# The last products of a stage in parts of the tokens, their norms and consumers part by part; the inverse's z times V with 128 columns

## The chip, the cores and the metric

The kernel runs on one core of one Trainium2 chip, as one program of some 56,700 instructions on the engines. The metric is the device time of one execution in microseconds (us): the median of the runs shown below. The engines are named as in the profile: PE is TensorE's matmuls and PEld its weight loads, DVE is VectorE, ACT ScalarE, POOL GpSimd, SP SyncE, which issues the DMAs.

## The reference, cut to what matters

Two residual blocks with adaptive norms work on 512 latent tokens and 256 context tokens of width 1024:

```python
def modulate(x, shift, scale):
    return rms_norm(x) * (1.0 + scale) + shift

def squared_relu_mlp(h, w1, w2):
    return jnp.square(jax.nn.relu(h @ w1)) @ w2
...
        h_l = modulate(x, sh_a, sc_a)
        h_c = modulate(ctx, csh_a, csc_a)
        if layer % 2 == 0:
            o_l, o_c = ab_mixer(h_l, h_c, ...)
        else:
            o_l, o_c = rwkv_mixer(h_l, h_c, ...)
        x = x + gt_a * o_l
        x = x + gt_m * squared_relu_mlp(modulate(x, sh_m, sc_m), mlp_w1[layer], mlp_w2[layer])
        if need_ctx:
            ctx = ctx + cgt_a * o_c
            ctx = ctx + cgt_m * squared_relu_mlp(modulate(ctx, csh_m, csc_m), mlp_w1[layer], mlp_w2[layer])
```

Layer 0 mixes with neighbourhood attention and an mLSTM (ab_mixer), layer 1 with an RWKV7 scan (rwkv_mixer), whose context output is not needed. A second block with another context follows (its mixer, and a mixture of experts), which the change touches at its first norm only. Every mixer ends in a product with a 1024x1024 matrix, every MLP in one with 4096x1024; its result is added to x, and the next stage begins with the norm of the new x.

## The kernel before, in words

All activations stand transposed: x is eight tiles (k = 0 to 7) of 128 features x 768 tokens, the latents in columns 0 to 511, the context in 512 to 767. `PARTS` is these two ranges, `LAT` the first alone. The stages follow each other: ab_mixer (its last products are called po), mlp(0) (products up and dn), rw_mixer (first products rp, the scan, last products ro), mlp(1) (latents only: up, dn), second_block (first products p).

A weight tile is 128 outputs x 1024 inputs in f32. `load_w` (L479) fetches it with a DMA into one of three buffers (wraw) and splits it into a rounded part wh on ACT (L476) and the rest wl on POOL (L477), each with two buffers. `dense` (L489) then runs, for each of the eight k, three products (wh with the activation's high part, wh with its low part, wl with the high part), each over every range of `parts`: 48 matmuls for `PARTS`, 24 for `LAT`. `dense_pair` does the first two weights of a stage at once, k by k, because its activations appear tile by tile.

The last products of a stage: for each output tile f, `dense`, then `residual` on DVE (L589, x += ps * gate) and `squares_add`: a square on ACT (L544) and the sum over f in acc (L546), on POOL for all f but the last. `rstd_tokens` sums acc over the partitions on PE (ssc, L554) and takes the reciprocal root (rsv, rst, rsy; L518 to L534); `rstd_banks` spreads it over the partitions by six products (rstd, L564). `modulate` then makes, k by k, modt on DVE (L579), ah on ACT (L581) and al on DVE (L582); these feed the pair of the next stage. In rw_mixer `shift` stands there: x scaled in place on DVE (L1138), shifted on ACT (L1140), and the sum of the two neighbouring tokens xx on POOL (L1141, with an edge copy on either side, L1142 and L1143); `tiles` makes the products' tiles from x and xx.

In rw_mixer the scan inverts 64x64 matrices block by block; the l-th step multiplies z with V (L1669): the weights are `U[:, c, :]`, 64 columns of f16, for each of 12 matrices c.

The order of instructions on each engine is set when the program is built: the code is written stage by stage, and a scheduler places the instructions of all engines by its own model of their times. Each engine then runs its list in order and waits at semaphores.

## Time and profile before

| | |
|---|---|
| median of 3 runs | 3540.41 us (3536.74 to 3541.11) |
| the profiled execution | 3541.96 us, its span 3540.1 us |
| PE busy | 3200.3 us (90%), 23582 matmuls |
| DVE, ACT, POOL busy | 1822.3 us (51%), 1321.4 us (37%), 910.1 us (26%) |
| wh on ACT, wl on POOL | 259 each, 1032 and 2410 ns |
| PE busy in 530 to 578 us (po) | 48.00 of 48 us, granted clock 1.00 |
| PE busy in 578 to 608 us (norm 1) | 23.16 of 30 us, clock 0.77 |
| PE busy in 1152 to 1194 us (norm 2) | 26.34 of 42 us, clock 0.72 |
| PE busy in 2233 to 2256 us (norm 3) | 16.34 of 23 us, clock 0.78 |
| PE busy in 2632 to 2664 us (norm 4) | 26.38 of 32 us, clock 0.79 |

PE is nearly always busy in the dense stretches, and pauses at the norms between two stages. The four norms that the change touches are numbered in order of time: 1 after po, 2 after dn of mlp(0), 3 after ro, 4 after dn of mlp(1). The granted clock is the share of TensorE's full speed that it ran at.

### The profile page before, as it was taken

What the parts mean: (1) busy time and instruction counts of PE and PEld (TensorE: products, weight loads), DVE (VectorE), ACT (ScalarE), POOL (GpSimd) and SP (SyncE); (2) the same over time, 40 slices, a digit from 0 to 9 for tenths busy, and PEclk for the clock granted to TensorE, in tenths of its full rate; (3) what the DMA queues carried; (4) which work ended last, traced back from release to release, by engine and by line L of the source; (5) the groups of instructions that cost most, each with busy time, mean ns of one, the idle gap of its engine ahead of it and who ended that gap; (6) DMA issues with size and microseconds to landing.
All of it is one profiled execution on the core that took longest, in us unless ns stands there. A gap on an engine that the chain in (4) does not pass through costs nothing. (4 is left out here: it accounts for less than half of the span.)

```text
span 3540.1 us, 56694 instructions
## 1 busy us (share of the span) xinstructions
PE 3200.3 (90%) x23582; PEld 2423.1 (68%) x23582; DVE 1822.3 (51%) x3073; ACT 1321.4 (37%) x2503; POOL 910.1 (26%) x467
## 2 busy tenths in 40 slices
PE   7989999999999789589999998899999989799887
PEld 4666887788888677377777786677878767433333
DVE  5476664852322975477777763774342564222213
ACT  3333453221222543377777775322233453100001
POOL 1111113222223423422222221444442324200000
PEclk9999999999999899699999998999999999899999
DMA  5222222551112223200000003474231227799997
GB/s 219 96 71 84 84 78 90 198 176 61 65 60 97 84 106 109 69 18 27 27 28 27 27 8 105 154 245 136 95 124 54 78 81 247 261 426 426 426 427 321
DMA packets 126321, 488.44 MB, mean 138 GB/s; under 512 B 13360, under 2 KB 23024, under 8 KB 101744
## 3 DMA queue, kind: packets, MB, share of 16 engines
q1 hardware_dynamic: 119936, 477.25, 36.6%
q8 instruction: 186, 3.05, 0.3%
q10 hardware_dynamic: 4944, 3.36, 0.3%
q0 software_dynamic: 1184, 4.20, 0.3%
q14 instruction: 71, 0.58, 0.0%
HBM read 455.92 MB, written 28.84 MB: 137 GB/s over the span
## 5 line engine op out<-in xcount | busy, mean ns | idle before, releaser
L477 POOL TENSOR_TENSOR wl<-w,wh 128x1024 fp32r<-128x1024 f32 (+1 forms) x259 | 623.5, 2410 | 1614.1 <-ACT wh L476 1461.6
L476 ACT ACTIVATE wh<-w 128x1024 fp32r<-128x1024 f32 (+1 forms) x259 | 266.9, 1032 | 920.3 <-PE dn L498 335.6
L498 PE MATMUL dn<-hh,wh 128*128 128x512 f32 (+1 forms) x768 | 236.4, 362 | 15.1 <-ACT hh L476 15.1
L498 PE MATMUL up<-ah,wh 128*128 128x512 f32 (+1 forms) x768 | 236.9, 364 | 6.5 <-ACT ah L581 2.8
L498 PE MATMUL up<-ah,wl 128*128 128x512 f32 (+1 forms) x768 | 236.6, 362 | 6.1 <-POOL wl L477 5.9
L498 PE MATMUL dn<-hl,wh 128*128 128x512 f32 (+1 forms) x768 | 236.7, 362 | 2.2 <-DVE hl L477 2.2
L498 PE MATMUL dn<-hh,wl 128*128 128x512 f32 (+1 forms) x768 | 235.8, 361 | 1.1 <-POOL wl L477 1.1
L498 PE MATMUL up<-al,wh 128*128 128x512 f32 (+1 forms) x768 | 236.6, 362 | 0.2 <-DVE al L582 0.2
L465 DVE SCALAR_TENSOR_TENSOR side<-wside,condb 128x1024 f32<-128x1024 f32 x128 | 193.2, 1509 | 66.7 <-DMA wside<-ada 65.4
L621 DVE TENSOR_TENSOR u<-u 128x768 f32<-128x768 f32 (+1 forms) x64 | 126.7, 1982 | 133.4 <-ACT u L620 133.4
L589 DVE SCALAR_TENSOR_TENSOR x<-dn,ada,x 128x512 f32<-128x512 f32 x96 | 60.5, 658 | 260.4 <-PE dn L498 260.4
L498 PEld LDWEIGHTS dn<-hh,wh 128*128 128x128 f32 x768 | 128.5, 190 | 40.4 <-ACT hh L476 16.6
L498 PEld LDWEIGHTS up<-ah,wh 128*128 128x128 f32 x768 | 128.9, 191 | 32.5 <-ACT ah L581 3.9
L498 PEld LDWEIGHTS up<-ah,wl 128*128 128x128 f32 x768 | 128.3, 190 | 33.3 <-POOL wl L477 9.9
L498 PEld LDWEIGHTS dn<-hl,wh 128*128 128x128 f32 x768 | 128.4, 190 | 28.0 <-DVE hl L477 4.3
L498 PEld LDWEIGHTS up<-al,wh 128*128 128x128 f32 x768 | 129.0, 191 | 25.2 <-DVE al L582 1.4
L498 PEld LDWEIGHTS dn<-hh,wl 128*128 128x128 f32 x768 | 128.3, 190 | 25.7 <-POOL wl L477 2.0
L476 ACT ACTIVATE hh<-u 128x768 fp32r<-128x768 f32 (+1 forms) x64 | 47.3, 740 | 220.1 <-DVE u L621 220.1
L498 PE MATMUL p<-ah,wh 128*128 128x512 f32 (+1 forms) x320 | 118.7, 400 | 2.2 <-ACT ah L581 1.2
L498 PE MATMUL rp<-xl,wh 128*128 128x512 f32 x368 | 110.2, 364 | 10.2 <-DVE xl L477 10.2
L498 PE MATMUL rp<-xh,wh 128*128 128x512 f32 x368 | 110.1, 366 | 9.1 <-ACT xh L476 7.8
L498 PE MATMUL p<-ah,wl 128*128 128x512 f32 x320 | 113.6, 384 | 2.1 <-POOL wl L477 2.1
(623 smaller groups left out, 7459.7 us busy)
## 6 DMA issues: line engine op xcount, KB each, us to landing
w<-mlp SPq DMA_DIRECT2D x128, 512.0 KB, 3.5
wside<-ada SPq DMA_DIRECT2D x96, 512.0 KB, 3.8
ew<-e_gate SPq DMA_DIRECT2D x45, 1024.0 KB, 19.5
ew<-e_up SPq DMA_DIRECT2D x41, 1024.0 KB, 20.7
ew<-e_down SPq DMA_DIRECT2D x39, 1024.0 KB, 19.5
wada<-ada SPq DMA_DIRECT2D x48, 512.0 KB, 3.8
ewm<-e_up SPq DMA_DIRECT2D x18, 1024.0 KB, 19.6
ewm<-e_down SPq DMA_DIRECT2D x18, 1024.0 KB, 19.6
```

The source lines that it names most:

```text
L465: nc.vector.scalar_tensor_tensor(o, w, 1.0, cb[:, q, :], op0=ALU.mult, op1=ALU.mult, accum_out=out[:, f, q:q + 1])
L476: nc.scalar.activation(hi, src, AF.Copy)
L477: (eng or nc.vector).tensor_tensor(lo, src, hi.bitcast(F32), op=ALU.subtract)
L498: nc.tensor.matmul(ps[:, a:b], ww[:, 128 * k:128 * k + 128], aa[:, a:b], start=(first and k == 0 and q == 0), stop=(last and k == nk - 1 a ...
L589: self.nc.vector.scalar_tensor_tensor(x[:, a:b], ps[:, a:b], gt[:, f, q:q + 1], x[:, a:b], op0=ALU.mult, op1=ALU.add)
L621: nc.vector.tensor_tensor(u[:, lo:hi], u[:, lo:hi], u[:, lo:hi], op=ALU.mult)
```

## The change

The last products of the four stages run part by part: all eight f for the first part, then all eight for the second. At po and dn of mlp(0) the parts are the latents and the context (`PARTS`), at ro and dn of mlp(1) the two halves of the latents (`HALVES`). So each of those weights is loaded and split twice. Each part has its own squares (the sums of 256 columns on DVE instead of POOL), ssc, rsqrt and rstd; those of the first part stand in the second part's products. `dense_pair`, `modulate`, and shift and tiles of rw_mixer (now `first_tiles`) go through a first part of all k, then the second. At norm 4 the context's norm is done ahead of the dn products. x is saved to DRAM for rw_mixer's end after the first part of mlp(0)'s last products, and its latents only. Two small constants move from a tile of the whole program to one of ab_mixer. In the scan, V has 13 matrices instead of 12, and z times V takes `U[:, c:c + 2]`, 128 columns, as weights; of the 128 partitions of its result 64 are read, as before.

```diff
+HALVES = ((0, T // 2), (T // 2, T))
...
+    def spill_x(self, part):
+
+        if part[0] < T:
+            for k in range(KD):
+                self.nc.sync.dma_start(self.dxs[k], self.x[k][:, :T])
...
         ps = [self.wide(name) for _ in srcs]
-        for k in range(n // 128):
-            for p, w in zip(ps, ws):
-                self.dense(p, [t[:, 128 * k:128 * k + 128] for t in w], act, parts, k0=k, first=(k == 0), last=(k == n // 128 - 1))
+        for part in parts:
+            for k in range(n // 128):
+                for p, w in zip(ps, ws):
+                    self.dense(p, [t[:, 128 * k:128 * k + 128] for t in w], act, [part], k0=k, first=(k == 0),
+                               last=(k == n // 128 - 1))
...
-    def modulate(self, tiles, sh, sc1, parts, pool):
+    def modulate(self, tiles, sh, sc1, pool):
...
+        for n, ((a, b), r) in enumerate(self.r.items()):
+            q = int(a >= T)
+            for k in range(KD):
+                t = pool.tile([128, TT], F32, tag="tmp", name=self.uid("modt"), bufs=self.tb)
+                if n == 0:
+                    out.append([pool.tile([128, TT], F32R, tag=tag, name=self.uid(tag), bufs=KD) for tag in ("ah", "al")])
+                h, l = out[k]
+                nc.vector.scalar_tensor_tensor(t[:, a:b], tiles[k][:, a:b], sc1[:, k, q:q + 1], r,
                                                op0=ALU.mult, op1=ALU.mult)
                 nc.scalar.activation(h[:, a:b], t[:, a:b], AF.Identity, bias=sh[:, k, q:q + 1])
                 nc.vector.scalar_tensor_tensor(l[:, a:b], t[:, a:b], sh[:, k, q:q + 1], h[:, a:b].bitcast(F32),
                                                op0=ALU.add, op1=ALU.subtract)
...
+    def residual_parts(self, name, product, gt, parts, acc, tmp, step=None, hook=None):
+
+        y = None
+        for n, part in enumerate(parts):
+            for f in range(KD):
+                ps = product(n, f, part)
+                self.residual(self.x[f], ps, gt, f, [part])
+                self.squares_add(acc, self.x[f], f, [part], tmp, self.nc.gpsimd if part[1] - part[0] > 256 else None)
+                if step:
+                    step()
+                if n and f == 1:
+                    self.r[parts[0]] = self.rstd_banks(y, parts[:1])[0]
+            y = self.rstd_tokens(acc, [part])
+            if hook:
+                hook(part)
+        self.r[parts[1]] = self.rstd_banks(y, parts[1:])[0]
...
+                    if layer == 1:
+
+                        for k in range(KD):
+                            self.squares_add(acc, self.x[k], k, PARTS[1:], tmp)
+                        self.r[PARTS[1]] = self.rstd_banks(self.rstd_tokens(acc, PARTS[1:]), PARTS[1:])[0]
+
+                    def product(n, f, part):
+                        ps = self.wide("dn")
+                        self.dense(ps, self.load_w(w2[g, f], 1024), hid, [part])
+                        return ps
+
+                    self.residual_parts("dn", product, gt, nparts, acc, tmp, next_side, hook)
+                    break
...
-            for f in range(KD):
+
+            def product(n, f, part):
                 ps = self.wide("po")
-                self.dense(ps, self.load_w(wo[f], 1024), act2, PARTS)
-                self.residual(self.x[f], ps, self.ada[0, 2], f, PARTS)
-                self.squares_add(acc, self.x[f], f, PARTS, tmp, nc.gpsimd)
-            self.y = self.rstd_tokens(acc, PARTS)
+                self.dense(ps, self.load_w(wo[f], 1024), act2, [part])
+                return ps
+
+            self.residual_parts("po", product, self.ada[0, 2], PARTS, acc, tmp)
...
-                for k in range(KD):
-                    nc.sync.dma_start(spill["x"][k], self.x[k])
...
+                def shift(k, q):
+                    h, s = hs[k], xx[k]
+                    for a, b in PARTS[q:q + 1]:
                         nc.vector.scalar_tensor_tensor(h[:, a:b], self.x[k][:, a:b], sc[:, k, q:q + 1], r[q],
                                                        op0=ALU.mult, op1=ALU.mult)
                         nc.scalar.activation(h[:, a:b], h[:, a:b], AF.Identity, bias=sh[:, k, q:q + 1])
                         (nc.gpsimd if k else nc.vector).tensor_tensor(s[:, a + 1:b - 1], h[:, a:b - 2], h[:, a + 2:b], op=ALU.add)
                         nc.gpsimd.tensor_copy(s[:, a:a + 1], h[:, a + 1:a + 2])
                         nc.gpsimd.tensor_copy(s[:, b - 1:b], h[:, b - 2:b - 1])
...
+                def first_tiles():
+
+                    out = []
+                    for q, (a, b) in enumerate(PARTS):
+                        n = 0
+                        for k in range(KD):
+                            while n < min(k + 3, KD):
+                                shift(n, q)
+                                n += 1
+                            t = pool.tile([128, TT], F32, tag="tmp", name=self.uid("xs"), bufs=self.tb)
+                            if q == 0:
+                                out.append(pair())
+                            h, l = out[k]
+                            nc.scalar.activation(t[:, a:b], hs[k][:, a:b], AF.Copy, scale=m2[:, 1, k:k + 1])
+                            nc.vector.scalar_tensor_tensor(t[:, a:b], xx[k][:, a:b], m2[:, 0, k:k + 1], t[:, a:b],
+                                                           op0=ALU.mult, op1=ALU.add)
+                            self.split(t[:, a:b], h[:, a:b], l[:, a:b])
+                    return out
...
-                first = self.dense_pair("ro", [wo[0], wo[1]], act, LAT, ws)
+                first = self.dense_pair("ro", [wo[0], wo[1]], act, HALVES[:1], ws)
...
+                self.residual_parts("ro", product, gt, HALVES, acc, tmp)
...
-                    nc.tensor.matmul(pz[:64, 64 * (c - a):64 * (c - a) + 64], U[:, c, :],
+                    nc.tensor.matmul(pz[:, 64 * (c - a):64 * (c - a) + 64], U[:, c:c + 2, :].rearrange("p c t -> p (c t)"),
                                      zb[:, c].rearrange("p h (b x w) -> p h b x w", x=2, w=w)[:, :, :, 1, :],
...
-        k.mlp(0, PARTS)
+        k.mlp(0, PARTS, PARTS, k.spill_x)
         k.rw_mixer()
-        k.mlp(1, PARTS[:1])
+        k.mlp(1, PARTS[:1], HALVES)
```

Line numbers of the changed kernel: L502 matmul of dense, L480 wh and other ACT splits, L481 wl, L546 and L550 squares on ACT, L552 acc, L524 to L540 rsqrt, L586 and L589 modulate, L596 residual, L1074 to L1149 the mLSTM head. Three places of the order follow. First PE, while the last mLSTM head finishes (ho are its last products, which need hsum from DVE; ch and cl are the activations of po, of which tile 7 needs ho). Before:

```order
L498 MATMUL po_4651<-ch_4555,wl_4655 128x512
L498 MATMUL po_4651<-ch_4555,wl_4655 128x256
L498 MATMUL po_4651<-ch_4559,wh_4654 128x512
L1103 MATMUL ho_4533<-consts,hsum_4489 128x128 x3
L498 MATMUL po_4651<-ch_4559,wh_4654 128x256
L1103 MATMUL ho_4533<-consts,hsum_4489 128x128
L1103 MATMUL ho_4539<-consts,hsum_4489 128x128
L498 MATMUL po_4651<-cl_4560,wh_4654 128x512
L1103 MATMUL ho_4539<-consts,hsum_4489 128x128
L498 MATMUL po_4651<-cl_4560,wh_4654 128x256
L498 MATMUL po_4651<-ch_4559,wl_4655 128x512
```

and the same place of the change:

```order
L502 MATMUL po_4644<-ch_4585,wh_4647 128x512
L502 MATMUL po_4644<-cl_4586,wh_4647 128x512
L502 MATMUL po_4644<-ch_4585,wl_4648 128x512
L1149 MATMUL ho_4551<-consts,hsum_4507 128x128 x4
L1149 MATMUL ho_4557<-consts,hsum_4507 128x128 x2
L502 MATMUL po_4610<-ch_4589,wh_4613 128x512
L502 MATMUL po_4644<-ch_4589,wh_4647 128x512
L502 MATMUL po_4610<-cl_4590,wh_4613 128x512
L502 MATMUL po_4610<-ch_4589,wl_4614 128x512
```

Before, 84 po matmuls of both widths (f0 and f1, k 0 to 6) stand ahead of or around ho; in the change it is 42 of 512 columns, all of them ahead, and behind ho come the products that need tile 7. Second DVE at norm 1, from the last residuals of po to the first modulated tiles. Before:

```order
L589 SCALAR_TENSOR_TENSOR x_4581<-po_4951,ada_2_356,x_4581 128x256
L589 SCALAR_TENSOR_TENSOR x_4582<-po_5011,ada_2_356,x_4582 128x512
L589 SCALAR_TENSOR_TENSOR x_4582<-po_5011,ada_2_356,x_4582 128x256
L546 TENSOR_TENSOR acc_4591<-acc_4591,sq_5068 128x768
L518 TENSOR_SCALAR rsv_5078<-ssc_5071 128x6
L527 RECIPROCAL rsy_5079<-rst_5081 128x6
L531 TENSOR_TENSOR rst_5081<-rsy_5079 128x6
L532 TENSOR_TENSOR rst_5081<-rst_5081,rsv_5078 128x6
L533 TENSOR_SCALAR rst_5081<-rst_5081 128x6
L534 TENSOR_TENSOR rsy_5079<-rsy_5079,rst_5081 128x6
L579 SCALAR_TENSOR_TENSOR modt_5104<-x_4575,ada_4_357,rstd_5096 128x512
L579 SCALAR_TENSOR_TENSOR modt_5104<-x_4575,ada_4_357,rstd_5101 128x256
```

and the change:

```order
L596 SCALAR_TENSOR_TENSOR x_4599<-po_5118,ada_2_374,x_4599 128x256
L552 TENSOR_TENSOR acc_4609<-acc_4609,sq_5150 128x256
L596 SCALAR_TENSOR_TENSOR x_4600<-po_5153,ada_2_374,x_4600 128x256
L552 TENSOR_TENSOR acc_4609<-acc_4609,sq_5185 128x256
L524 TENSOR_SCALAR rsv_5191<-ssc_5188 128x2
L586 SCALAR_TENSOR_TENSOR modt_5214<-x_4593,ada_4_375,rstd_4973 128x512
L533 RECIPROCAL rsy_5192<-rst_5194 128x2
L586 SCALAR_TENSOR_TENSOR modt_5220<-x_4594,ada_4_375,rstd_4973 128x512
L537 TENSOR_TENSOR rst_5194<-rsy_5192 128x2
L589 SCALAR_TENSOR_TENSOR al_5216<-modt_5214,ada_3_376,ah_5215 128x512
L538 TENSOR_TENSOR rst_5194<-rst_5194,rsv_5191 128x2
```

In the change the second part's residuals and sums follow one another, and the first modulation of 512 columns (modt_5214, which needs rstd of the first part only) stands behind the last sum and rsv of the second part. Third ACT at norm 4, where dn of mlp(1) begins. Before:

```order
L620 ACTIVATE u_25824<-up_25793 128x512
L476 ACTIVATE hh_25825<-u_25824 128x512
L476 ACTIVATE wh_25903<-w_25901 128x1024
L540 ACTIVATE acc_25831<-x_23186 128x768
L541 ACT_TABLE_LOAD
L541 ACTIVATE warm<-acc_25831 128x1
L476 ACTIVATE wh_25938<-w_25936 128x1024
L544 ACTIVATE sq_25898<-x_23187 128x768
```

and the change:

```order
L649 ACTIVATE u_26439<-up_26408 128x512
L546 ACTIVATE acc_26446<-x_23428 128x256
L550 ACTIVATE sq_26449<-x_23429 128x256
L547 ACT_TABLE_LOAD
L547 ACTIVATE warm<-acc_26446 128x1
L480 ACTIVATE hh_26440<-u_26439 128x512
L550 ACTIVATE sq_26452<-x_23430 128x256
L550 ACTIVATE sq_26455<-x_23431 128x256
L550 ACTIVATE sq_26458<-x_23432 128x256
L550 ACTIVATE sq_26461<-x_23433 128x256
L550 ACTIVATE sq_26464<-x_23434 128x256
L480 ACTIVATE wh_26558<-w_26556 128x1024
```

The squares of the context tiles (all of 256 columns, acc_26446 to sq_26464) now stand ahead of wh_26558, the third weight of dn.

## Rows read from the trace of the kernel before

**Rows 1.** Timeline of PE at the start of po (start, duration, work, [idle <-releaser]).

```profile
519.59 0.62 PE L1103 MATMUL ho<-consts,hsum 128*128 128x128 f32 x3
```

**Rows 2.** Timeline of DVE: residuals of po, then of dn of mlp(1).

```profile
569.83 1.14 DVE L589 SCALAR_TENSOR_TENSOR x<-po,ada,x 128x512 f32<-128x512 f32 x2 [7.34 <-PE po L498]
...
578.31 1.14 DVE L589 SCALAR_TENSOR_TENSOR x<-po,ada,x 128x512 f32<-128x512 f32 x2 [7.34 <-PE po L498]
...
2592.07 0.75 DVE L589 SCALAR_TENSOR_TENSOR x<-dn,ada,x 128x512 f32<-128x512 f32 x1 [0.82 <-PE dn L498]
...
2597.67 0.75 DVE L589 SCALAR_TENSOR_TENSOR x<-dn,ada,x 128x512 f32<-128x512 f32 x1 [4.85 <-PE dn L498]
```

**Rows 3.** Timeline of ACT and POOL: one weight's split during po.

```profile
569.52 1.06 ACT L476 ACTIVATE wh<-w 128x1024 fp32r<-128x1024 f32 x1 [6.15 <-PE po L498]
...
570.66 2.40 POOL L477 TENSOR_TENSOR wl<-w,wh 128x1024 fp32r<-128x1024 f32 x1 [4.29 <-ACT wh L476]
```

**Rows 4.** Timelines at norm 1.

```profile
579.14 2.35 POOL L477 TENSOR_TENSOR wl<-w,wh 128x1024 fp32r<-128x1024 f32 x1 [4.29 <-ACT wh L476]
...
580.43 1.87 DVE L546 TENSOR_TENSOR acc<-acc,sq 128x768 f32<-128x768 f32 x1 [0.98 <-ACT sq L544]
...
582.35 2.72 PE L554 MATMUL ssc<-ones,acc 128*128 128x2 f32 x12 [4.08 <-DVE acc L546]
...
587.75 1.80 DVE L579 SCALAR_TENSOR_TENSOR modt<-x,ada,rstd 128x512 f32<-128x512 f32 x3 [1.21 <-PE rstd L564]
...
607.75 1.06 ACT L476 ACTIVATE wh<-w 128x1024 fp32r<-128x1024 f32 x1 [2.79 <-PE up L498]
```

**Rows 5.** Groups by form, 588 to 606 us (count | busy us, mean ns | idle).

```profile
L582 DVE SCALAR_TENSOR_TENSOR al<-modt,ada,ah 128x512 fp32r<-128x512 f32 x8 | 6.0, 746 | 0.0
...
L582 DVE SCALAR_TENSOR_TENSOR al<-modt,ada,ah 128x256 fp32r<-128x256 f32 x8 | 3.8, 479 | 0.0
...
L581 ACT ACTIVATE ah<-modt,ada 128x256 fp32r<-128x256 f32 x8 | 4.0, 500 | 2.9 <-DVE modt L579 2.8
```

**Rows 6.** Timelines at norm 2.

```profile
1151.71 1.14 DVE L589 SCALAR_TENSOR_TENSOR x<-dn,ada,x 128x512 f32<-128x512 f32 x2 [7.33 <-PE dn L498]
...
1171.03 1.03 POOL L1141 TENSOR_TENSOR xx<-x 128x510 f32<-128x510 f32 x1
...
1173.81 0.61 POOL L1141 TENSOR_TENSOR xx<-x 128x254 f32<-128x254 f32 x1
...
1174.61 1.03 POOL L1141 TENSOR_TENSOR xx<-x 128x510 f32<-128x510 f32 x1
...
1193.80 1.06 ACT L476 ACTIVATE wh<-w 128x1024 fp32r<-128x1024 f32 x1 [3.12 <-PE rp L498]
```

**Rows 7.** Timelines at norm 3.

```profile
2232.46 0.75 DVE L589 SCALAR_TENSOR_TENSOR x<-ro,ada,x 128x512 f32<-128x512 f32 x1 [4.69 <-PE ro L498]
...
2255.60 1.06 ACT L476 ACTIVATE wh<-w 128x1024 fp32r<-128x1024 f32 x1 [6.04 <-issue]
```

**Rows 8.** Timelines at norm 4 and in its products.

```profile
2593.72 1.28 ACT L541 ACT_TABLE_LOAD   x1
...
2631.26 0.75 DVE L589 SCALAR_TENSOR_TENSOR x<-dn,ada,x 128x512 f32<-128x512 f32 x1 [4.85 <-PE dn L498]
...
2663.29 1.06 ACT L476 ACTIVATE wh<-w 128x1024 fp32r<-128x1024 f32 x1 [2.97 <-PE p L498]
```

**Rows 9.** Lines L1669 and L1635 (duration min/median/max), and their timeline.

```profile
L1669 PEld LDWEIGHTS <-V x960: 106/113/177, 1481.2 to 2128.9; 128*64 128x64 f16 x192
...
L1635 PEld LDWEIGHTS <-zb x384: 95/98/152, 1476.1 to 2131.0; 128*128 128x128 f16 x192
...
1515.22 0.44 PE L1669 MATMUL i<-zb,V 128*64 128x64 f16 x8
...
1503.33 0.52 PE L1635 MATMUL i<-crwh,zb 128*128 128x64 f16 x12
```

**Rows 10.** Timeline of POOL in mlp(0), two wl in a row.

```profile
608.94 5.96 POOL L477 TENSOR_TENSOR wl<-w,wh 128x1024 fp32r<-128x1024 f32 x2 [27.46 <-ACT wh L476]
```

More of the change, by code (lines that the diff above doesn't have):

```diff
@@ L334, in __init__ @@
         nc.vector.memset(self.eps, 1e-6)
+        dr = ctx.enter_context(tc.tile_pool(name="x_d", bufs=1, space=bass.MemoryType.DRAM))
+        self.dxs = [dr.tile([128, T], F32, name=f"d_x{k}") for k in range(KD)]
         self.warm = self.const.tile([128, 1], F32, name="warm")
@@ L597, in mlp @@
         with tc.tile_pool(name=f"mlp{layer}", bufs=2, reuse_waits="tile") as pool:
+            for tag, dt, bufs in (("hh", F32R, 10), ("hl", F32R, 10)):
+                pool.tile([128, TT], dt, tag=tag, name=self.uid(tag), bufs=bufs)
             side = self.ada_side(layer + 1, pool)
@@ L626, in up, with next_side @@
                 return hid
+            def next_side():
+                if side:
+                    side.pop(0)()
             if layer == 1:
@@ L1122, in rw_mixer @@
             H = {n: crh[:, a:b] for n, (a, b) in self.crwh.items()}
-            spill = {n: [dr.tile([128, TT], F32, name=f"d_{n}{f}") for f in range(8)] for n in ("x", "r", "k", "kk", "v", "g", "o")}
+            spill = {n: [dr.tile([128, TT], F32, name=f"d_{n}{f}") for f in range(8)] for n in ("r", "k", "kk", "v", "g", "o")}
             tw = [cp.tile([128, TT], F32R, name=f"tw{z}") for z in range(2)]
@@ L1341, in rw_scan @@
             hi=[diag(f"hi{i}", dt=F16) for i in range(2)], zb=[diag(f"zb{i}", dt=F16) for i in range(2)], lo=diag("lo", dt=F16),
-            V=[pool.tile([128, 12, 64], F16, name=f"V{l}", bufs=1) for l in range(1, 6)],
+            V=[pool.tile([128, 13, 64], F16, name=f"V{l}", bufs=1) for l in range(1, 6)],
             C=C, H=H, tw=tw, ta=ta, pool=pool, n=0)
```

109 lines of the change are left out of this document (45 added, 64 removed).

## The prediction

> **What bounds the kernel now.** The kernel is a chain of dense stages, so I first read the timeline of the engines around the four norms that the change touches. In a dense stretch TensorE never waits: one 128x1024 weight over 768 tokens takes 8.48 us (569.83 to 578.31, two results apart), one over 512 tokens 5.60 us (2592.07 to 2597.67) [rows 2]. So the 256 context tokens of a weight cost 2.88 us. The supply of weights has slack there: ScalarE makes the high half (wh) as soon as TensorE frees a buffer, at 569.52, GpSimd the low half (wl) from 570.66 to 573.06 [rows 3], 3.54 us after the release and well inside 8.48 or 5.60.
>
> At a norm the chain breaks. The last residual of the first one starts at 578.31 [rows 2]; the last addition of squares waits behind GpSimd, the statistics start on TensorE at 582.35, the first modulated tile at 587.75, and the pair of products after it gives its first buffer back at 607.75 [rows 4]: 29.4 us for 17.0 us of products. The other three, from the last residual to that release: 42.1 us [rows 6], 23.1 us [rows 7], 32.0 us [rows 8].
>
> **What the change costs: the products.** Every weight of the four stages comes twice, and the second pass runs over 256 tokens only. With two buffers a release starts wh and wl (3.54 us), and 22 of 24 matmuls still follow from the first that needs wl (2.88 x 22/24 = 2.64 us): 6.18 us for two weights, 3.09 for one, against 2.88 us of work. In order:
> - Norm 1 (po): 8 such weights x 0.21 = 1.7 us. The statistics of the first part stand 19 matmuls into the next weight, in front of the other 29, and need GpSimd's addition first; by their count they take two thirds of the 2.72 us of all twelve [rows 4], some of it under the running matmuls: I take 1.4 us. And the run-ahead shrinks: while the last mLSTM head finishes, until ho at 519.59 [rows 1] and somewhat beyond, TensorE works on po f0 and f1, 84 matmuls of both widths before, 42 of 512 columns after (the order above). The 42 of 256 columns, 42 x 0.12 = 5.0 us, come later. Sum 8.1 us.
> - Norm 2 (dn of mlp0): 1.7 + 1.4 = 3.1 us.
> - Norm 3 (ro): sixteen half-weights at 3.09 instead of 5.60/2 = 2.80: 4.6 us; and a square of 0.50 [rows 5] and a table load of 1.28 us [rows 8], with a small operation, go ahead of the third wh: 2.0 us. Sum 6.6 us.
> - Norm 4 (dn of mlp1): 4.6 us, and five squares of the context norm, 5 x 0.50 [rows 5], with a table load, ahead of the third wh: 3.8 us. Sum 8.4 us.
>
> **What it gives: from the products' end to the pair's end.** The order shows that VectorE modulates the first part only behind the last addition and rsv of the second. So the chain stays, with smaller steps, counted from the last residual's start: the residual (0.48 us), a square, the addition. Today's addition starts at 580.43 and takes 1.87 us; GpSimd's wl beside it ends at 581.49 [rows 4], 3.2 us after the residual's start, and the addition 0.81 later. I let the new one of 256 columns wait for wl too, until 3.2 + 0.4 = 3.6 us; a third of the statistics, 0.9 us, and rsv: modulation starts at 4.8 us. After it VectorE sets the pace: 16 operations of 0.75 and 16 of 0.48 us [rows 5] are 19.7 us.
> - Norm 1: 4.8 + 19.7 + 0.3 = 24.8 us against 29.4: -4.6.
> - Norm 3: 32 operations of 0.48: 4.8 + 15.3 + 0.8 = 20.9 against 23.1: -2.2.
> - Norm 4: 48 of 0.48, and 1.0 us of small operations for the router: 4.8 + 1.0 + 22.9 + 0.5 = 29.2 against 32.0: -2.8.
> - Norm 2: here GpSimd paces the pair. Of a tile's 3.58 us, 2.78 are the 510-wide sum with its two edge copies and 0.80 the 254-wide one with its own (starts at 1171.03, 1173.81, 1174.61) [rows 6]. The scaling of the latents now runs inside the context products, which hides it, but GpSimd's sums stand behind its last wl in the order, 3.2 us after the residual. Seven latents tiles (VectorE sums tile 0) 7 x 2.78 = 19.5, eight of context 6.4, and 1.8 for the last split and its products: 30.9 against 42.1: -11.2.
>
> **The inverse's z.** 960 products load V as 64 columns: 113 ns a load against 98 for 128 columns; in a row they start 36 ns apart ((0.44 - 0.19)/7), those with 128 columns 30 ns ((0.52 - 0.19)/11) [rows 9]. The bounds are nothing (the chain through zb waits anyway) and 15 ns x 960 = 14.4 us; I take the starts, 6 ns x 960 = -5.8 us, because loads lie under other products. At nothing the time would be 3546 us, which the forecast's own range below holds. [...] The trace has the load of 128 columns 15 ns shorter, so by it something is left.
>
> The rest costs nothing that I can find: 32 more loads of weights lie beside products that run at the pace of the splits, and the moved constants and the smaller spill of x beside products as well; without that cover a load would be late once, about as long as one split (3.5 us).
>
> **Sum.** 8.1 + 3.1 + 6.6 + 8.4 = +26.2; -4.6 - 11.2 - 2.2 - 2.8 = -20.8; z -5.8: -0.4 us on the profiled execution, which took 3541.96 us. It lies 1.55 above the median of the runs, so I forecast 3540 us, and 3533 to 3547 if the mechanism is as told. A measurement of this kernel tells about 0.2%, 7 us, from no change.
>
> **Rivals.**
> - VectorE and GpSimd get out of each other's way. GpSimd's two edge copies in a 510-wide step cost 2.78 - 1.03 = 1.75 us [rows 6] though a copy moves one column; if VectorE's smaller operations let them run in a quarter of it, GpSimd needs 1.5 us a tile instead of 2.78, TensorE's 17 us of products become the limit, and norm 2 gains 6 more. If the addition slips in ahead of wl (ready at some 1.5 us, wl starts at 0.8), each norm gains 2.0, 8 in all. 3540 - 14 = 3526 us. For it: beyond wl, an addition of 768 columns needed only 0.81 us. Against: wl starts first. Chance 0.26.
> - z gives its whole load difference: 8.6 more, 3531 us. For it: the scan's products are short. Against: they already overlap their loads. Chance 0.08.
> - Slower, by one mechanism: wl itself becomes longer. Where VectorE squares u beside it, two take 5.96 us, 2.98 each instead of 2.40 [rows 10]. Squares are now added by VectorE from two tiles in SBUF, once per weight. If that costs wl 0.58 us, two weights cost that much more, and 46 weights (8, 8, 14 and 16) 46 x 0.29 = 13.3: 3553 us. It decides from 0.3 us on each wl. Against: the addition fits into GpSimd's gap between one wl and the next release. Chance 0.18. [...]
> - The change doesn't do what it says: since modulation stays behind the last rsv, norms 1, 3 and 4 keep their length from the last residual on, and the -9.6 goes: 3550 us. For it: the order of VectorE. Against: twelve statistics become four. Chance 0.14.
>
> **How the numbers follow.** The forecast has 0.34. Faster: 0.26 + 0.08 = 0.34. Slower: 0.18 + 0.14 = 0.32. The range reaches over the bulk of the rivals on both sides: 3522 (the first, with half of the second's 8.6) to 3557 (3553 with one late load); each side leaves about 0.1 out. The forecast's own range is the 3533 to 3547 above.
>
> **What would show it.** Right: 256-wide residuals of the second pass 3.0 to 3.2 us apart; TensorE idle for some 5 us around the last ho; modulation 5 us after the last residual, at all but norm 2; GpSimd's sums back to back there; 25, 31, 21 and 29 us from last residual to first release; z products 30 ns apart. Wrong: residuals 2.9 us apart (then supply is free, 10 us less) or 3.4 (the longer wl); sums on GpSimd under 2 us a tile; first products within 4 us of the last residual. What I can't price from this trace is how TensorE's clock answers to shorter pauses; a pair that VectorE paces hides most of it.

## The result and the profile after

The changed kernel takes 3566.24 us (median of 4 runs, 3563.57 to 3572.52) against 3540.76 for the kernel before, measured beside it: 1.0077 times as long, with an interval of 1.0065 to 1.0089. That is slower by 25 us, above the range of 3522 to 3557. The profiled executions differ by 21.6 us (3563.57 and 3541.96), and those are taken apart below. Two runs of the experiments, 10446.03 us in e12_z96 and 12230.37 us in e14_sel2, took some three times as long as the others of their kernels and are left out of the medians given.

The page of the changed kernel, its span and the busy time of each engine:

```profile
span 3561.7 us, 58071 instructions
## 1 busy us (share of the span) xinstructions
PE 3190.8 (90%) x24062; PEld 2448.0 (69%) x24062; DVE 1925.6 (54%) x3214; ACT 1364.4 (38%) x2617; POOL 967.5 (27%) x487
```

It does not say where the time went. For that I took the start of the same event (a stage's last residual, a pair's first release, the first and the last product of the inverse) from both traces, and the difference of each stretch, after minus before, in us. As in the prediction, the last residual before is the 512-column one of the last tile; its 256-column one starts 0.67 us later. The experts' stage counts from its first product.

| stretch | forecast | measured |
|---|---|---|
| norm 1: up to the last residual; from there to the release | +8.1; -4.6 | +13.5; -4.6 |
| mlp(0) up to its last up | 0 | -6.2 |
| norm 2: the same two | +3.1; -11.2 | +11.2; -8.5 |
| scan, first to last product of the inverse (659.8 to 638.1) | -5.8 | -21.8 |
| norm 3 | +6.6; -2.2 | +15.0; -0.2 |
| norm 4 | +8.4; -2.8 | +18.1; -1.9 |
| stretches between these; experts' stage, to the end | 0; 0 | +0.2; +6.7 |

The products by parts cost 57.8 us where 26.2 stood in the sum; behind them 15.2 came back of 20.8; the scan gave 21.8 instead of 5.8.

**Norm 1** (timelines of the changed kernel; these answer to [rows 1], [rows 2] and [rows 4]):

```profile
518.88 1.22 PE L1149 MATMUL ho<-consts,hsum 128*128 128x128 f32 x6 [2.09 <-DVE hsum L1142]
521.81 1.22 PE L502 MATMUL po<-ch,wh 128*128 128x512 f32 x2 [1.72 <-ACT ch L480]
...
527.24 0.80 PE L502 MATMUL po<-ch,wl 128*128 128x512 f32 x1 [0.67 <-POOL wl L481]
...
562.95 2.37 POOL L481 TENSOR_TENSOR wl<-w,wh 128x1024 fp32r<-128x1024 f32 x1 [1.97 <-ACT wh L480]
563.51 2.35 DVE L552 TENSOR_TENSOR acc<-acc,sq 128x512 f32<-128x512 f32 x1 [0.77 <-ACT sq L550]
565.92 1.05 PE L560 MATMUL ssc<-ones,acc 128*128 128x2 f32 x8 [1.71 <-DVE acc L552]
...
572.07 0.48 DVE L596 SCALAR_TENSOR_TENSOR x<-po,ada,x 128x256 f32<-128x256 f32 x1 [3.21 <-PE po L502]
573.40 2.42 DVE L552 TENSOR_TENSOR acc<-acc,sq 128x256 f32<-128x256 f32 x1 [0.84 <-ACT sq L550]
575.75 0.47 DVE L596 SCALAR_TENSOR_TENSOR x<-po,ada,x 128x256 f32<-128x256 f32 x1
...
573.14 2.40 POOL L481 TENSOR_TENSOR wl<-w,wh 128x1024 fp32r<-128x1024 f32 x1 [1.99 <-ACT wh L480]
...
591.85 0.47 DVE L596 SCALAR_TENSOR_TENSOR x<-po,ada,x 128x256 f32<-128x256 f32 x1
...
596.17 0.74 DVE L586 SCALAR_TENSOR_TENSOR modt<-x,ada,rstd 128x512 f32<-128x512 f32 x1
...
616.70 1.06 ACT L480 ACTIVATE wh<-w 128x1024 fp32r<-128x1024 f32 x1 [2.63 <-PE up L502]
```

The addition of 256 columns begins at 573.40, 0.26 us into GpSimd's wl of 573.14, and ends 0.28 us behind it. The next residual follows at once. So it goes with each weight of the pass, and with the statistics of the first part: their last addition (563.51) lasts as long as the wl beside it (562.95), and TensorE stands still 1.71 us. Short pauses like this one can be followed by a lower granted clock, as the windows of the changed kernel show (PE, PEld, DVE, ACT, POOL busy, then PEclk):

```profile
523.00:529.00 6.00, 5.25 (x12) 3.22 (x12) 1.50 (x2) 3.14 (x5) 4.18 (x2) 0.50 0.35 87
...
562.00:567.00 5.00, 3.29 (x28) 3.08 (x27) 3.10 (x2) 1.41 (x2) 2.37 (x1) 1.00 0.25 69
567.00:572.00 5.00, 5.00 (x31) 5.00 (x31) 1.39 (x7) 1.77 (x4) 2.37 (x1) 0.66 0.24 90
...
753.40:758.40 5.00, 4.99 (x29) 4.44 (x30) 3.43 (x5) 0.00 (x0) 1.03 (x1) 1.00 0.87 301
...
1152.00:1156.00 4.00, 4.00 (x25) 4.00 (x24) 2.34 (x5) 2.00 (x4) 1.77 (x1) 0.62 0.72 206
...
2181.00:2186.00 5.00, 5.00 (x24) 5.00 (x25) 0.00 (x0) 0.10 (x1) 2.24 (x1) 0.51 0.69 188
2593.50:2602.00 8.50, 5.92 (x28) 5.72 (x29) 4.32 (x10) 0.20 (x1) 2.40 (x1) 0.62 0.43 123
```

In five rows the granted clock is 0.50 to 0.66. It is 0.50 (half clock, below) from 523 to 529 us throughout, and from 568 to 571 in the row of 0.66, where products of 256 columns start 0.21 us apart; at 1.00, from 562 to 564 us, they start 0.12 apart. Pauses stand before these rows or in them: 2.09, 1.72 and 0.67 us round the last ho, 1.71 us for the statistics, 1.93 to 3.44 us in the rows below. But a pause alone does not decide it: behind one of 2.46 us, which ends at 753.41 in mlp(0), the clock is 1.00.

**Norm 2** (these answer to [rows 6]): a wait for wl inside the second pass, GpSimd's sums in the pair, and a wait of GpSimd between those of the latents and those of the context.

```profile
1151.28 0.38 PE L502 MATMUL dn<-hh,wl 128*128 128x256 f32 x1 [1.94 <-POOL wl L481]
...
1165.75 0.47 DVE L596 SCALAR_TENSOR_TENSOR x<-dn,ada,x 128x256 f32<-128x256 f32 x1
...
1176.61 1.56 POOL L1188 TENSOR_TENSOR xx<-x 128x510 f32<-128x510 f32 x1
...
1179.38 1.50 POOL L1188 TENSOR_TENSOR xx<-x 128x510 f32<-128x510 f32 x1
...
1186.64 0.18 POOL L1189 COPY xx<-x 128x1 f32<-128x1 f32 x1 [2.38 <-ACT x L1187]
...
1189.88 0.60 POOL L1188 TENSOR_TENSOR xx<-x 128x254 f32<-128x254 f32 x1
...
1191.11 0.61 POOL L1188 TENSOR_TENSOR xx<-x 128x254 f32<-128x254 f32 x1
...
1199.39 1.06 ACT L480 ACTIVATE wh<-w 128x1024 fp32r<-128x1024 f32 x1 [1.28 <-PE rp L502]
```

**Norms 3 and 4** (these answer to [rows 7] and [rows 8]): the pair that opens the half pass of ro ends with two residuals in one row, and the next comes 11.3 us later.

```profile
2174.79 0.88 DVE L596 SCALAR_TENSOR_TENSOR x<-ro,ada,x 128x256 f32<-128x256 f32 x2 [3.53 <-PE ro L502]
...
2177.45 1.99 ACT L480 ACTIVATE wh<-w 128x1024 fp32r<-128x1024 f32 x2
...
2178.54 0.38 PE L502 MATMUL ro<-oh,wh 128*128 128x256 f32 x1 [3.44 <-ACT wh L480]
...
2180.97 0.58 PE L502 MATMUL ro<-oh,wl 128*128 128x256 f32 x1 [1.93 <-POOL wl L481]
...
2186.05 0.48 DVE L596 SCALAR_TENSOR_TENSOR x<-ro,ada,x 128x256 f32<-128x256 f32 x1 [8.05 <-PE ro L502]
...
2591.13 5.92 DVE L552 TENSOR_TENSOR acc<-acc,sq 128x256 f32<-128x256 f32 x4
...
2596.77 1.01 PE L560 MATMUL ssc<-ones,acc 128*128 128x2 f32 x4 [2.58 <-DVE acc L552]
...
2602.29 0.48 DVE L596 SCALAR_TENSOR_TENSOR x<-dn,ada,x 128x256 f32<-128x256 f32 x1 [3.09 <-PE dn L502]
```

At norm 3 TensorE stops 3.44 and 1.93 us, and the whole next stretch is at 0.51. At norm 4 four additions take 5.92 us, three of them of the context norm and two of these held by a wl on GpSimd each (2.57 and 2.39 us, the other two 0.43 and 0.42); TensorE waits 2.58 us for them with the statistics in front of its other products.

### The profile page after: what moved, and what is told of

The parts are those of the page before. It is cut to its first block, busy times and chain, and to the rows that moved or that the text cites. A ratio compares the mean times of both kernels' runs of the same rounds, so it can differ in the third digit from the quotient of the medians.

```text
span 3561.7 us, 58071 instructions
## 1 busy us (share of the span) xinstructions
PE 3190.8 (90%) x24062; PEld 2448.0 (69%) x24062; DVE 1925.6 (54%) x3214; ACT 1364.4 (38%) x2617; POOL 967.5 (27%) x487
## 5 line engine op out<-in xcount | busy, mean ns | idle before, releaser
L481 POOL TENSOR_TENSOR wl<-w,wh 128x1024 fp32r<-128x1024 f32 (+1 forms) x291 | 704.0, 2421 | 1596.0 <-ACT wh L480 1493.0
L480 ACT ACTIVATE wh<-w 128x1024 fp32r<-128x1024 f32 (+1 forms) x291 | 300.5, 1034 | 888.4 <-PE dn L502 315.3
L502 PE MATMUL dn<-hh,wh 128*128 128x512 f32 (+1 forms) x832 | 259.9, 350 | 18.0 <-ACT hh L480 17.3
L502 PE MATMUL dn<-hh,wl 128*128 128x512 f32 (+1 forms) x832 | 259.8, 350 | 9.3 <-POOL wl L481 9.2
L502 PE MATMUL dn<-hl,wh 128*128 128x512 f32 (+1 forms) x832 | 259.1, 349 | 2.7 <-DVE hl L481 2.7
L502 PE MATMUL up<-ah,wh 128*128 128x512 f32 (+1 forms) x784 | 238.9, 356 | 9.3 <-ACT ah L588 4.2
L502 PE MATMUL up<-ah,wl 128*128 128x512 f32 (+1 forms) x784 | 240.4, 356 | 5.5 <-POOL wl L481 5.5
L502 PE MATMUL up<-al,wh 128*128 128x512 f32 (+1 forms) x784 | 239.7, 355 | 0.8 <-DVE al L589 0.8
L502 PE MATMUL rp<-xs,wh 128*128 128x512 f32 (+1 forms) x736 | 189.7, 363 | 16.8 <-DVE xs L481 9.1
L596 DVE SCALAR_TENSOR_TENSOR x<-dn,ada,x 128x512 f32<-128x512 f32 (+1 forms) x104 | 62.8, 623 | 212.6 <-PE dn L502 212.6
L502 PEld LDWEIGHTS dn<-hh,wh 128*128 128x128 f32 x832 | 148.2, 194 | 40.0 <-ACT hh L480 19.5
L502 PEld LDWEIGHTS dn<-hh,wl 128*128 128x128 f32 x832 | 147.9, 194 | 32.4 <-POOL wl L481 12.7
L502 PEld LDWEIGHTS dn<-hl,wh 128*128 128x128 f32 x832 | 148.0, 194 | 24.7 <-DVE hl L481 5.1
L502 PEld LDWEIGHTS rp<-xs,wh 128*128 128x128 f32 x736 | 124.7, 193 | 44.0 <-DVE xs L481 12.8
L502 PEld LDWEIGHTS up<-ah,wh 128*128 128x128 f32 x784 | 132.7, 191 | 31.5 <-ACT ah L588 4.5
L502 PEld LDWEIGHTS up<-ah,wl 128*128 128x128 f32 x784 | 132.8, 191 | 30.1 <-POOL wl L481 9.2
L502 PEld LDWEIGHTS up<-al,wh 128*128 128x128 f32 x784 | 132.6, 190 | 23.1 <-DVE al L589 1.9
L480 ACT ACTIVATE hh<-u 128x768 fp32r<-128x768 f32 (+1 forms) x64 | 47.3, 740 | 223.4 <-DVE u L650 223.4
L502 PE MATMUL p<-ah,wh 128*128 128x512 f32 (+1 forms) x336 | 123.4, 389 | 3.4 <-ACT ah L588 2.0
L552 DVE TENSOR_TENSOR acc<-acc,sq 128x256 f32<-128x256 f32 (+2 forms) x59 | 108.9, 1848 | 30.5 <-ACT sq L550 29.6
```

Source lines behind the costliest of these rows:

```text
L480: nc.scalar.activation(hi, src, AF.Copy)
L481: (eng or nc.vector).tensor_tensor(lo, src, hi.bitcast(F32), op=ALU.subtract)
L502: nc.tensor.matmul(ps[:, a:b], ww[:, 128 * k:128 * k + 128], aa[:, a:b], start=(first and k == 0 and q == 0), stop=(last and k == nk - 1 a ...
L552: eng.tensor_tensor(acc[:, lo:hi], acc[:, lo:hi], sq[:, lo:hi], op=ALU.add)
L596: self.nc.vector.scalar_tensor_tensor(x[:, a:b], ps[:, a:b], gt[:, f, q:q + 1], x[:, a:b], op0=ALU.mult, op1=ALU.add)
```

## The experiments

The theory after the result: dividing the products costs what the rows above show, through GpSimd's wl and the pauses with half clock behind them, and the part-wise consumers bring little; z and what goes with it gives the whole gain. The rivals: the consumers give a gain that only the halves of norms 3 and 4 eat; the scan's gain is that of the constants' new place; VectorE's held additions are themselves the pace. Ratios are to the kernel before.

**The constants alone, and with z.** In the kernel before, hsel and hbc go into the first block's table and sel2 is dropped (e2_const); then z takes V on 128 columns too (e1_constz), for which the 13th block of V needs the room that the constants leave.

```
-                nc.tensor.matmul(pz[:64, 64 * (c - a):64 * (c - a) + 64], U[:, c, :],
+                nc.tensor.matmul(pz[:, 64 * (c - a):64 * (c - a) + 64], U[:, c:c + 2, :].rearrange("p c t -> p (c t)"),
```

> The kernel before with the two small constants moved from the program's tile to ab_mixer's, and nothing else. Theory A (the moved tile shifts the addresses of all later tiles, and that is why a 512-column matmul of the two-part stages starts its successor after 228 instead of 235 ns in the changed kernel): the same 228 ns here, some 6 to 10 us faster, about 3532. Rival B (the new order of the hidden tiles in mlp does it): 235 ns, 3541. Rival C (the moved constants are also why the scan is 22 us shorter): 3519.

> The kernel before with the moved constants (without them V does not fit) and z times V on 128 columns. Theory A (the 128-column z alone shortens the scan by the 22 us seen, because TensorE's granted clock no longer dips in it): 20 to 24 us less than with the constants alone, about 3511, granted clock 1.00 from 1550 us to the scan's end. Rival B (z gives the 5.8 us that I forecast, and parts of x or other moved tiles give the rest): 6 us less than with the constants alone, dips of the clock as before.

e2_const: 3535.25 us, 0.9987 (0.9978 to 0.9997). e1_constz: 3518.71, 0.994 (0.9923 to 0.9956). The medians differ by 16.5 us, the profiled executions by 21.8 (that of e1_constz is the quickest of its four). The scan takes 660.4 us with the constants alone and 638.4 with z, so its gain is z's. The window over most of the scan, first e2_const, then e1_constz:

```profile
1500.00:2100.00 600.00, 555.75 (x9001) 468.81 (x9000) 431.08 (x821) 437.74 (x1114) 154.62 (x76) 0.97 0.08 24
```

```profile
1500.00:2100.00 600.00, 552.22 (x9320) 470.64 (x9320) 438.19 (x846) 453.55 (x1154) 156.37 (x76) 0.99 0.08 24
```

In the same 600 us TensorE gets through 3.5% more products (9320 for 9001), at a granted clock of 0.99 for 0.97. In stretches of 40 us the mean is 0.994 for 0.970: from 1540 on, 9 of 14 are below 1.00 with 64 columns, none with 128 (nor in the changed kernel). A mean lower by 0.024 over 600 us is 14 us of work at full clock (0.024 x 600), so without the dips at most 14 of the 22.0 us are had, an estimate.

That is a bound. What dips cost is shown by other kernels with the same z on 128 columns whose scan did dip: two or three of the 14 stretches in e10_pad, e13_hbm, e6_latestat and e7_dvewl (scan 642.8 to 642.9 us), four in e8_pooladd (643.6), none in five, the changed kernel among them (638.0 to 640.2). The four cost 5.5 us against the changed kernel and take the mean clock of the whole scan, by the traces' clock records, from 0.981 to 0.968. In e2_const it is 0.959; by this rate the clock gives 9 to 10 of the 22.0 us, an estimate.

The rest is in the products. The twelve ahead of z and the first of z, in e2_const and in e1_constz:

```profile
1502.95 0.45 PE L1658 MATMUL i<-V,zb 128*128 128x32 f16 x12 [0.32 <-DVE V L1652]
1503.33 0.44 PE L1664 MATMUL i<-zb,V 128*64 128x64 f16 x8
```

```profile
1504.17 0.45 PE L1658 MATMUL i<-V,zb 128*128 128x32 f16 x12 [0.33 <-DVE V L1652]
1504.47 0.40 PE L1664 MATMUL i<-zb,V 128*128 128x64 f16 x8
```

With 64 columns the first z product starts 0.38 us after the twelve begin, with 128 columns 0.30: the turn from the last of the twelve takes 106 ns (median), or 25. The scan has 64 such turns, 5.2 us. And z products in a row start 35 ns apart with 64 columns at full clock, 30 with 128; from start to next start all 960 take 42.9 and 37.6 us, 5.3 less.

**The parts taken back.** In the changed kernel the last products run whole at all four norms (e3_whole), or at norms 3 and 4 only (e4_whole34).

```
+    def residual_whole(self, name, product, gt, parts, acc, tmp, step=None, hook=None):
...
+        for f in range(KD):
+            ps = product(0, f, parts)
+            self.residual(self.x[f], ps, gt, f, parts)
+            self.squares_add(acc, self.x[f], f, parts, tmp, self.nc.gpsimd)
...
+        y = self.rstd_tokens(acc, parts)
...
-            self.residual_parts("ro", product, gt, HALVES, acc, tmp)
+            self.residual_whole("ro", product, gt, LAT, acc, tmp)
```

> The changed kernel with the last products of all four stages over all parts at once again, each weight loaded once; norms, sums on GpSimd and statistics as before; modulation and pairs still part by part, the context's norm at norm 4 still ahead. Theory A (products in two passes cost 58 us in pauses, half clock behind them and slower supply, and give back 14 us after the products): 44 us less than the changed kernel, 3522, or less by what the consumers in parts give. Rival B (only the supply costs, 3.2 instead of 2.8 or 2.9 us on 46 weights, 17 us; the rest is contention of the whole program): 3553.

> The changed kernel with the last products of the third and fourth stage (the halves of the latents) over whole tiles again; the first two stages in parts. Theory A: norms 3 and 4 give back 15.8 + 17.9 - 1.7 = 32 us: 3534. Rival B (supply alone, 16 x 0.4 us in each): 13 us, 3553.

e3_whole: 3529.78 us, 0.9968 (0.9954 to 0.9983), 36 less than the changed kernel. In its trace the products at the four norms are 54.3 us shorter, and 13.0 are lost behind them. e4_whole34: 3535.65, 0.9985 (0.9975 to 0.9994), 30.6 less; the table has 31.0 for norms 3 and 4. That these agree is in part chance: in its trace the two norms give back 27.6 us, and 5.0 come from the stages behind norm 4. With norms 1 and 2 in parts the kernel is 6 us slower than with none. And e3_whole, with the part-wise consumers but whole products, is 11 us above e1_constz: they bring nothing by themselves. In its trace 4.8 us of that arise in dn of mlp(1), where the context norm stands ahead now. From the last residual (here the very last) to the first release e3_whole has 28.7 us at norm 1 where e1_constz has 27.5, and 31.3 at norm 4 like e1_constz.

**What paces the second pass.** Three edits of the changed kernel: the statistics of both parts together at the end (e6_latestat); wl of the second pass on VectorE (e7_dvewl); the additions of 256 columns on GpSimd (e8_pooladd).

```
-        self.split(w, h, l, nc.gpsimd)
+        self.split(w, h, l, eng or nc.gpsimd)
...
-                self.dense(ps, self.load_w(wo[f], 1024), act2, [part])
+                self.dense(ps, self.load_w(wo[f], 1024, nc.vector if n else None), act2, [part])
```

```
-                self.squares_add(acc, self.x[f], f, [part], tmp, self.nc.gpsimd if part[1] - part[0] > 256 else None)
+                self.squares_add(acc, self.x[f], f, [part], tmp, self.nc.gpsimd)
```

> The changed kernel with the statistics of both parts taken together behind the last product (ssc, rsqrt, rstd of the first part no longer in the second part's products). Theory A (TensorE pauses some 1.7 us there for an addition that VectorE can't do beside GpSimd's wl, and then runs at half clock): the first two or three tiles of the second pass come 3.2 us apart instead of 4 to 6; 3 us less in products at norms 1, 3 and 4, 8 at norm 2, where the scaling of the latents leaves the products too but comes back behind them; 8 to 12 us less than the changed kernel in all, some 3556. Rival B (the supply of weights alone sets the pace of the second pass): no change, 3566.

> The changed kernel with wl of the second pass made by VectorE instead of GpSimd. Theory A (supply through GpSimd at 3.2 us a tile, VectorE's additions held by it): tiles of 256 columns at 2.8 to 2.9 us, additions of 0.4 to 0.5 instead of 1.9 us, 10 to 15 us less than the changed kernel, some 3553. Rival B (the pauses at the start of each pass make the loss, the pace in between costs little): 3566 less 3.

> The changed kernel with the second pass's sums of squares on GpSimd, as the first pass has them, the last one on VectorE. Theory A (the 1.85 us that VectorE's additions of 256 columns take beside wl are waiting of VectorE alone and delay nothing on TensorE but the last one): no change, 3566 within 4 us, though VectorE is 60 to 100 us less busy. Rival B (they hold up the residuals and so the products): 8 us or more less.

e7_dvewl: 3544.29 us, 1.0009 (0.9997 to 1.0022), 22 less than the changed kernel, more than the 10 to 15 of its theory A. Its products are 4.7, 8.0, 3.5 and 4.7 us shorter at the four norms, 20.9 together. VectorE's timeline in its second pass of po:

```profile
574.84 1.23 DVE L481 TENSOR_TENSOR wl<-w,wh 128x1024 fp32r<-128x1024 f32 x1 [0.49 <-ACT wh L480]
575.99 0.42 DVE L552 TENSOR_TENSOR acc<-acc,sq 128x256 f32<-128x256 f32 x1
576.72 0.48 DVE L596 SCALAR_TENSOR_TENSOR x<-po,ada,x 128x256 f32<-128x256 f32 x1 [0.31 <-PE po L502]
...
579.56 0.48 DVE L596 SCALAR_TENSOR_TENSOR x<-po,ada,x 128x256 f32<-128x256 f32 x1 [0.26 <-PE po L502]
```

The same wl takes 1.23 us there instead of 2.40, the same addition 0.42 instead of 2.2 to 2.4, and the residuals stand 2.84 apart, at the 2.88 us of work: supply through GpSimd, with the additions that it holds up, was the pace. The group of all additions, in the changed kernel and then in e7_dvewl:

```profile
L552 DVE TENSOR_TENSOR acc<-acc,sq 128x256 f32<-128x256 f32 (+2 forms) x59 | 108.9, 1848 | 30.5 <-ACT sq L550 29.6
```

```profile
L552 DVE TENSOR_TENSOR acc<-acc,sq 128x256 f32<-128x256 f32 (+2 forms) x59 | 61.3, 1041 | 17.9 <-ACT sq L550 16.9
```

So an addition of 256 columns takes 0.42 us alone, and up to 2.57 with a wl on GpSimd. In the changed kernel each one that begins beside a wl ends 0.28 to 0.29 us behind it, at all four norms. In e7_dvewl it takes 0.42 us at 584.58, with no wl on GpSimd, and 2.40 at 586.59, beside GpSimd's wl of 586.33 (2.38 us).

e8_pooladd: 3566.53 us, 1.0077 (1.0056 to 1.0099), as the changed kernel. VectorE no longer waits, but GpSimd has 2.40 us of wl and 0.74 of addition for each weight, and the residuals stand 3.2 apart as before. So freeing VectorE gains nothing if GpSimd gets the addition. What VectorE's being held costs by itself this run does not show, because GpSimd is now busy for 3.14 of each 3.2 us. In the changed kernel GpSimd stands idle 0.7 to 0.9 us before each wl of the pass, mostly for wh.

e6_latestat: 3563.04 us, 1.0075 (1.0051 to 1.0098), 3 less, which is within the intervals, where its theory A had 8 to 12. The products become 5.5, 7.4, 2.1 and 3.2 us shorter, 18.2 together: the price of the early statistics with the half clock behind them, and at norm 2 of the scaling of the latents, which also leaves the products. Of it 3.0 us are lost again behind norm 1 and 6.4 behind norm 2, where all this comes at the end; 4.8 are lost in the scan, whose clock dips twice in this execution. The number at norm 1 counts from po's first residual, which comes 4.3 us later here. So it does in e4_whole34 (5.1), whose norm 1 is the changed kernel's and comes out 2.6 us shorter by that measure: so much of the 5.5 may be chance.

**Columns of z.** e1_constz with 96 columns instead of 128 (e12_z96).

```
-                nc.tensor.matmul(pz[:, 64 * (c - a):64 * (c - a) + 64], U[:, c:c + 2, :].rearrange("p c t -> p (c t)"),
+                nc.tensor.matmul(pz[:96, 64 * (c - a):64 * (c - a) + 64], U[:, c:c + 2, :].rearrange("p c t -> p (c t)")[:, :96],
```

> The kernel before with the moved constants and z times V on 96 columns of weights instead of 128. Theory A (only a full load of 128 columns is quick, and the quick loads end the dips of the clock): as with 64 columns, 3535, load near or above 113 ns, dips in the scan. Rival B (more columns of the array in use end the dips, quick load or not): no dips, 3520 to 3525.

3529.60 us, 0.9972 (0.9961 to 0.9984), between the two theories; the scan takes 653.0 us, and 4 of the 14 stretches of 40 us are below 1.00. The loads (minimum, median, maximum in ns), of the changed kernel and of e12_z96; they answer to [rows 9]:

```profile
L1729 PEld LDWEIGHTS <-V x960: 95/97/151, 1486.8 to 2113.0; 128*128 128x128 f16 x192
```

```profile
L1664 PEld LDWEIGHTS <-V x960: 119/125/204, 1468.3 to 2108.9; 128*96 128x96 f16 x192
```

By columns the median load is 113 ns with 64, 125 with 96, 97 with 128: of the larger two only the load of 128 columns takes less than that of 64, by 16 ns. Fewer dips than with 64 columns (6 to 9 of 14 in four kernels) came with slower loads, so the dips don't go with the load's time. Whether they go with the columns is less sure: kernels with 128 columns have none to four, and e8_pooladd, with four like e12_z96, has a scan of 643.6 us for 653.0. What tells 96 from 128 columns is the products themselves: z products start 45 ns apart with 96, for 30; the turn into them takes 25 ns with either.

**Eight bytes.** The constants had moved two stages that they don't touch: mlp(0) became quicker and the experts' stage slower, in e2_const as in the changed kernel. Kernels for that: the kernel before without sel2 only, which is 8 bytes a partition (e14_sel2); e1_constz with its constants in HBM as before (e13_hbm); e1_constz with an unused tile of 288 columns from the second block on (e10_pad), or of 290 (e15_pad290), which makes up all of the 1160 bytes by which the constants shrank, where 288, against what its expectation says, leaves 8; and the kernel before once more (c_before).

```
+            pad = st.enter_context(self.tc.tile_pool(name="pad", bufs=1, reuse_waits="tile"))
+            pad.tile([128, 290], F32, name="pad")
```

> The kernel before with the moved constants and the 128-column z, and an unused tile of 1152 bytes a partition at the start of the second block, so that its tiles stand at the addresses they had before. Theory A (the shifted addresses of the experts' weight tiles take the DMAs of the last stage from 426 to 421 GB/s): 426 GB/s from 3100 to 3400 us, some 5 us less than without the unused tile, 3513. Rival B (the rate is lower for another reason): 421 GB/s, 3518.

> The kernel before once more, for a second profile of it. Theory A (the DMA rate of the last stage and the dips of TensorE's clock in the scan belong to the kernel): 426 GB/s from 3100 to 3400 us, dips as before. Rival B (both are of the one execution): 421 GB/s, or no dips.

> The kernel before with the moved constants and the 128-column z, but the constant tables in HBM as in the kernel before (only the tiles in SBUF are the new ones). Theory A (the layout of the inputs in HBM takes the experts' DMAs from 426 to 421 GB/s): 426 GB/s, some 5 us less than without it, 3514. Rival B (the SBUF addresses do): 421 GB/s, 3519.

> The kernel before without the unused constant sel2, 8 bytes a partition, so that every later tile on that side stands 8 bytes lower. Theory A (the start of the matmul after a 512-column one after 235 instead of 228 ns comes from tiles that stand 8 bytes off a larger boundary): 228 ns, 3533 to 3535 as with all constants moved. Rival B (which tiles share a larger block of SBUF decides): 235 ns, 3541.

> The kernel before with the moved constants and the 128-column z, and an unused tile of 290 columns, 1160 bytes a partition, at the start of the second block: the whole shift, where the earlier one of 288 columns left 8 bytes of it. Theory A (8 bytes decide: tiles 8 bytes off a boundary take the experts' DMAs at 426 GB/s, tiles on it at 421): 426 GB/s, the last stage 5 us shorter, 3513 to 3514, the quickest kernel here. Rival B (not the addresses of the second block's tiles but something else that goes with the 8 bytes): 421 GB/s, 3518.

e14_sel2: 3536.67 us, 0.999 (0.998 to 1.0). e13_hbm: 3517.56, 0.9933 (0.9916 to 0.9949). e10_pad: 3520.24, 0.9955 (0.9941 to 0.997). c_before: 3538.39, one run. e15_pad290: 3511.72, 0.9919 (0.9898 to 0.9941), the quickest of all. DMA in the experts' stage, 3100 to 3400 us, in c_before, e14_sel2, e15_pad290:

```profile
DMA packets 17912, 127.90 MB, mean 426 GB/s; under 512 B 1990, under 2 KB 1990, under 8 KB 2630
```

```profile
DMA packets 17656, 126.00 MB, mean 420 GB/s; under 512 B 1965, under 2 KB 1965, under 8 KB 2605
```

```profile
DMA packets 17979, 127.86 MB, mean 426 GB/s; under 512 B 1998, under 2 KB 1998, under 8 KB 2766
```

e10_pad has 420, e13_hbm 421, the changed kernel 419: the tables' place in HBM is not it, and the 8 bytes by which e15_pad290 differs from e10_pad are enough, so the place in SBUF is. Two products of the second half of mlp(0), 256 and 512 columns in turn, in c_before and in e14_sel2:

```profile
980.25 0.52 PE L498 MATMUL dn<-hh,wh 128*128 128x512 f32 x2
980.61 0.52 PE L498 MATMUL dn<-hl,wh 128*128 128x512 f32 x2
```

```profile
980.46 0.51 PE L494 MATMUL dn<-hh,wh 128*128 128x512 f32 x2
980.81 0.51 PE L494 MATMUL dn<-hl,wh 128*128 128x512 f32 x2
```

## Why the prediction was wrong

**The step that failed** is the cost of the products: +26.2 stood for +57.8. Its count of supply was nearly right: 3.09 us a half-weight was forecast and 3.2 measured at norms 1, 3 and 4. What it lacked is in four places.
- The statistics of the first part had 1.4 us at norms 1 and 2, and nothing at norms 3 and 4. I let VectorE's addition wait for wl at the end of the products, and not here, inside them, where the last addition is VectorE's too and not GpSimd's, as I wrote; and I gave the pause no half clock. At norm 1 the residual behind the statistics comes 5.7 us after the one before it, at norm 2 5.9. e6_latestat prices all of it at 18.2 us, the next point at norm 2 included.
- At norm 2 I had the scaling of the latents hidden by the context products. Its eight operations stand among the residuals on VectorE, and the residuals come 2.8 to 5.0 us apart there behind the first of the pass.
- The pair that opens norm 3 gives both buffers back together. I counted its squares and table load (2.0 us), but the next weight also waits for wh and wl with nothing to cover them, and then runs at 0.51. The same place at norm 4 has additions of the context norm held by two wl. These two are read from the rows; no run took them alone.
- Half clock after the pauses in general. The prediction said that it could not price this; it should have widened the range upwards for it. No run takes it alone, so how the rest of the 57.8 us divides among these points stays open.

e7_dvewl and e6_latestat overlap (both shorten the statistics' wait), so their gains are not added up.

**Behind the products** -15.2 stood against -20.8. Norm 1 came out as worked out, with modulation 4.3 us after the last residual (4.8 forecast). Norm 2 missed 2.7 us, and not as forecast: the seven sums of 510 columns take 1.2 to 2.8 us a tile, 16.0 with their copies for 19.5; then GpSimd waits 2.38 us for the context's x, which the sum did not have; and the eight of 254 columns take 10.0 us for 6.4, most of them 1.23 with their copies instead of 0.80. Norms 3 and 4 missed 2.0 and 0.9 us: the chain is 4.6 and 5.4 us up to modulation, but then the pair takes longer than VectorE's operations alone. That the consumers' shorter chains are worth less than the passes cost is shown by e3_whole and e4_whole34.

**z** was mis-sized: -5.8 for -21.8, beyond its bound of -14.4. That bound had only the loads in it. The term itself came out: the starts are 30 ns apart, as forecast, and give 5.3 us. What it lacked is the turn into z, 5.2 us, and the scan's clock, 0.97 before, a row that I had not read for this stage: 9 to 10 us by the rate above. Some 2 us stay open.

**Nothing for the rest** was wrong twice, by -6.2 us in mlp(0) and +6.7 in the experts' stage. They nearly cancel.

**The rivals.** GpSimd's wl did not become longer (2.34 to 2.42 us beside an addition, once 2.54), so the rival of 3553 us had the right pair of operations and the wrong loser: VectorE is the one that waits, up to 2.57 us for an addition of 0.42. VectorE and GpSimd did not get out of each other's way: the additions begin behind wl and wait for it, though the first sums at norm 2 are short. z gave more than the rival with its whole load difference. The consumers did shorten, so the change does what it says.

## What to carry to other kernels

Before a pass is divided, take for the shorter pass every helper of a weight by itself: where one engine's share (here GpSimd's 2.40 us of 2.88) nearly fills the pass, each small operation that it holds up (here an addition of 0.42 us that takes up to 2.57), and each reduction put in the middle (here 1.71 us of pause at norm 1), can become a pause of TensorE, and the stretch after a pause is to be priced at half clock as well as at full (here 0.51 to 0.66 behind some pauses, 1.00 behind others). Read the granted clock of every stage that an edit touches, also when the edit is about something else. Take a change with several edits apart: here z with the moved constants was worth 21 us and the passes cost 36, and the sum told of neither.
